# Where the last two residual gates stand, and by how many products the last one is made

## Chip, cores and metric

One NeuronCore of a Trainium2 chip (trn2). The metric is device time in microseconds of one execution of the kernel; lower is better.

## The reference

One encoder layer on 2048 prompt tokens and 64 sample tokens, model width 1024, all in float32. Cut to what matters here:

```python
h = rms_norm(x, g_pre)
vA, bA, cA, zA, q, f, iv, zB, gA, gB = split_cols(h @ w_in)          # ten projections of 1024
yA = (silu(zA) * bA * causal_conv3(cA * vA)) @ w_a_out               # path A
o  = hgrn2_scan(S0, q, k(f), iv, log(fg(f)))                         # path B, chunks of 64
yB = (rms(o) * g_onorm * silu(zB)) @ w_b_out
out = (sigmoid(gA) * yA + sigmoid(gB) * yB) @ w_o
x = x + rms_norm(out, g_post)
gate = sigmoid(rms_norm(x, g_ple) @ w_ple_gate)                      # the residual gate, W_G
x = x + (p @ w_ple_proj) * gate                                      # PLE
```

The results are x, the last two columns of the convolution's input, and the scan's final states, for prompt and sample.

## The kernel before

The 2112 tokens are cut into three blocks of 768, 704 and 640 (`SIZES`), each with two halves (`segs`, 384, 352 and 320 columns). Everything is kept with features on the partitions and tokens in the free dimension, so a tile of a block is 128 x 768, 128 x 704 or 128 x 640, and eight tiles make the width of 1024. Float32 accuracy comes from splitting both operands into a high and a low part (`split`, line 230: a cast on ScalarE, a subtraction on VectorE) and three matmuls, hi·hi, hi·lo, lo·hi. Weights come from HBM as pieces of 256 KB (`load_raw`, on SP's queue). Their low part is either subtracted again or, where it has been stored before (`lows`), loaded with another 256 KB (`split_w`).

Most products of weights and activations are made by seven products instead of eight (Winograd's form of Strassen's method) over 2 x 2 pieces, with the sums S1 to S4 of the weights and T1 to T4 of the activations. There are two forms of this:

- `sgroup` (lines 457 to 459) takes two output blocks at a time, for the ten projections. Sums of the weights are made in the first block, kept in HBM (`sums`) and loaded in the others.
- `in_turn` (lines 608 to 610) makes product after product over four groups g, for W_A, W_B and W_O. The order of the products is `IN_TURN` or `IN_TURN_LATE`; the activations' sums for the next product are made while one runs (`operand_of`); a stage's `sink` takes each quarter of the output. `anew` names the weights whose low part is subtracted and not loaded. The weights' sums for these stages are made ahead by `prepare_sums`, in pieces hung between other work.

The residual gate, W_G, is made by plain products in all three blocks (`gemm`, `gemm_by_k`, lines 646 to 648). PLE is plain too (`ple`, lines 1318 to 1320).

A block runs through path B (eight heads, `path_b`), path A (`path_a`), W_A, W_B, W_O, the norm after W_O (`final_norm`), the gate (`final_gate`). `final_norm` sums squares of W_O's output, makes the first factor (`rms`: transposes on TensorE, a reduction, the power -0.5 on POOL in line 704, transposes back), adds x, makes the second factor likewise and multiplies by `g_ple`, which gives the gate's operand h.

Steps that should run beside matmuls are hung on hooks: `spread_out` gives plans of how many steps run after each group of matmuls. An instruction within `placed()` comes no earlier on its engine than the last matmul written before it. A DMA given to `paced` waits for that matmul. The remaining order on each engine is a planner's, by the order of writing, readiness and estimated costs. Large activation tiles share one ring of 48 (`rt`).

In the first and the middle block the norm is hung between the next block's first seven groups of projections (`LEAD`), and the gate follows right behind them, ahead of the next block's path B. In the last block there is no next block. There the norm is split by halves, each with its own factors; the first half's norm is begun within the last product of W_O and goes on beside PLE, and the second half's is hung between the first half's gate:

```python
norms = [final_norm(bl, [s], xo, acc, h2, None, s is segs[1]) for s in segs]
...
spread_out((norms[0], (2, 2, 1, 0, 1, 1, 4, 4)), (norms[1], (0,) * 6 + (1, 1) + (1, 1, 1, 0, 0, 1, 0, 1, 4, 4)))
run(ple(bl, ph, kept, spare=range(KB)))
run(gate[0], 2)
...
run(gate[1])
```

Of the kernel before, what the change touches and what calls it, by code (L numbers as in the profile page):

```python
# [18 lines left out]
P = 128  # L19
# [75 lines left out]
def hybrid_step(  # L95
# [193 lines left out]
    def load_w(idx, anew=False):  # L289

        parts = []
        for half_ in range(2):
            raw = load_raw(w_blk[idx, half_])
            with tc.high_priority():
                parts.append(split_w(raw, None if anew else (idx, half_)))
        return parts
# [3 lines left out]
    last, hooks, copies, adds, ahead, evicted, freed, powers, means = [None], [], [None], [None], [], [], [], [], []  # L300
# [31 lines left out]
    sums = {}  # L332
# [9 lines left out]
    def kept_w(i1, i2, name, anew=False, spread=False):  # L342
# [7 lines left out]
        return split_w(load_raw(sums[i1][name]), (i1, name))  # L350
# [24 lines left out]
    def prepare_sums(firsts, shared=False, pieces=False):  # L375
# [33 lines left out]
        for n, i1 in enumerate(firsts):  # L409
# [4 lines left out]
            if i1 >= W_O:  # L414
# [17 lines left out]
            if more and W_B <= i1 < W_O:  # L432
                nxt = load(firsts[n + 1])
# [3 lines left out]
            if more:  # L437
                if not W_B <= i1 < W_O:
                    nxt = load(firsts[n + 1])
                yield  # L440
# [132 lines left out]
    def in_turn(stages, operand):  # L573
# [15 lines left out]
        for i, (st, n) in enumerate(todo):  # L589
# [4 lines left out]
            for g in range(KH):  # L594
# [33 lines left out]
                elif what in ("p5", "p7"):  # L628
# [3 lines left out]
                    with behind_all(ahead):  # L632
                        V.tensor_tensor(p57, p57, t, ALU.add)
                        st["sink"](g, 1, 1, u2, p57)
# [18 lines left out]
    def gemm(idx, act, segs, anew=False):  # L653
# [23 lines left out]
    def gemm_by_k(idxs, act, segs, anew=False):  # L677
# [22 lines left out]
    def rstd_of(ms_ap, out_ap, scale):  # L700
        scaled = V.tensor_scalar(out_ap, ms_ap, scale, EPS, ALU.mult, ALU.add).ins
        means[:] = [scaled]
# [26 lines left out]
    def rms(acc, out, segs, hasten=False):  # L729
# [4 lines left out]
        for sg, col in zip(segs, cols):  # L734
            if hasten:
                ahead[:] = [V.tensor_copy(out[:, cols_of(sg)], spread(col, sg["n"])).ins]
            else:
                A.copy(out[:, cols_of(sg)], spread(col, sg["n"]))
# [490 lines left out]
    def path_b(bl, hc, first, kept, fills, hs, lead_sums=None):  # L1229
# [9 lines left out]
        for hd in range(NH):  # L1239
# [7 lines left out]
            piece = lead_sums and partial(next, lead_sums, None)  # L1247
# [162 lines left out]
    def out_in_turn(mg, xo, acc, last):  # L1410


        stage = dict(idx=W_O, order=IN_TURN if last else IN_TURN_LATE, raw=mg, anew=())
        if last:
            xo.extend(rt() for _ in range(KB))
        begun = set()

        def sink(g, c, h, x, y):
            if not last and c == 0 and h == 0:
                xo.append(rt())  # L1420
            v = half((xo if last or c == 0 else stage["mid"])[g + c * KH * last], h)
            into(v, x, y)
            if last:
                sum_squares(int(h in begun), v, half(acc, h), hn())
                begun.add(h)
# [4 lines left out]
    def final_norm(bl, segs, xo, acc, h2, kept, ask_ahead=False):  # L1430
# [3 lines left out]
        c = slice(segs[0]["off"], segs[-1]["off"] + hn())  # L1434
        n = len(segs) * hn()
        acc2, rs, rs2 = rt(), rt(), rt()
        xks = []

        def fetch():
            j = len(xks)  # L1440
            if j < KB:
                xks.append(rt())
                load = G.dma_start(xks[j][:, c], x_fm[j * P : (j + 1) * P, segs[0]["t0"] : segs[0]["t0"] + n])
                if not bl["last"]:
                    paced(load)

        if kept is not None:
            for j in range(KB):
                sum_squares(j, xo[j], acc, width[0])
                if j % 2:  # L1450
                    yield
        for _ in range(2):
            fetch()
            if kept is not None:
                yield
        for _ in rms(acc, rs, segs, bl["last"]):
            if kept is not None:
                fetch()
            yield
        if ask_ahead:  # L1460
            for _ in range(3):
                fetch()
                fetch()
                yield
        for j in range(KB):
            fetch()
            xj = xo[j][:, c]
            V.scalar_tensor_tensor(xj, xj, g_post[:, j : j + 1], rs[:, c], ALU.mult, ALU.mult)
            V.tensor_tensor(xj, xj, xks[j][:, c], ALU.add)

            for i in (j,) if not bl["last"] else (j - 1,) if 0 < j < KB - 1 else (j - 1, j) if j else ():
                sum_squares(i, xo[i][:, c], acc2[:, c], n)
            yield
        stored = iter(range(0 if kept is None else KB))
# [6 lines left out]
        for _ in rms(acc2, rs2, segs, bl["last"]):  # L1481
# [3 lines left out]
        for j in range(KB):  # L1485
            store(1)
            if len(h2) <= j:
                h2.append((rt(dt=F32R), rt(dt=F32R)))

            for i in (j, j + 1) if j == 0 else (j + 1,):  # L1490
                if i < KB:
                    ts.append(rt())
                    V.scalar_tensor_tensor(ts[i][:, c], xo[i][:, c], g_ple[:, i : i + 1], rs2[:, c], ALU.mult, ALU.mult)
            split(ts[j][:, c], h2[j][0][:, c], h2[j][1][:, c])
            yield

    def final_gate(bl, segs, xo, h2, kept, anew=False, held={}):

        late = []

        def merge(j, t, pj, xj):
            V.tensor_tensor(t[:, c], pj[:, c], t[:, c], ALU.mult)
            V.tensor_tensor(t[:, c], t[:, c], xj[:, c], ALU.add)
            (SP if bl["last"] and j >= KB - 2 else G).dma_start(y_fm[j * P : (j + 1) * P, segs[0]["t0"] : segs[0]["t0"] + len(segs) * hn()], t[:, c])

        c = slice(segs[0]["off"], segs[-1]["off"] + hn())
        for j in range(KB):
            if not bl["last"]:
# [313 lines left out]
```

## Time and profile before

| | |
|---|---|
| median of 3 runs | 2519.85 us (2516.96 to 2520.59) |
| profiled execution | 2516.69 us, its span 2515.0 us |
| TensorE (PE) busy | 2500.4 us, 99% |
| VectorE (DVE) busy | 1887.6 us, 75% |
| ScalarE (ACT) busy | 1491.5 us, 59% |
| GpSimd (POOL) busy | 481.0 us, 19% |
| DMA | 736.17 MB, mean 293 GB/s |

PE is matmuls, PEld weight loads, which overlap them. Lines such as L608 are lines of the kernel. A matmul is shown with its whole way through the pipeline, about 0.3 us for 320 columns, though the next one begins about 0.15 us after it; so the pace is read from starts. An arrow `<-` names what ended the wait before an instruction.

### The profile page before, as it was taken

The page shows a single profiled execution, that of the slowest core. Times are in us where ns is not written, and L with a number is a line of the kernel's source. Part 1 is how long each engine was busy: PE and PEld are TensorE (multiplying, and loading weights), DVE is VectorE, ACT ScalarE, POOL GpSimd, SP SyncE. Part 2 cuts the span into 40 slices and gives each one's busy share as a digit, 9 for nine tenths or more (in the row PEclk, how much of TensorE's full clock was granted, in tenths as well). Part 3 has the DMA queues.
Part 4 walks back from the last instruction along what each step waited for, and adds up shares of the span by engine and source line. Part 5 has one row for each costly group of instructions (what it writes and reads, how often), then busy time and mean ns, then how long its engine had stood idle before and what let it go on. Part 6 is the DMA issues. An engine that isn't in the chain of part 4 may idle for free.

```text
span 2515.0 us, 47257 instructions
## 1 busy us (share of the span) xinstructions
PE 2500.4 (99%) x16302; PEld 2481.1 (99%) x16302; DVE 1887.6 (75%) x3639; ACT 1491.5 (59%) x2902; POOL 481.0 (19%) x819
## 2 busy tenths in 40 slices
PE   9999999999999999999999999999999999999999
PEld 9999999999999999999999999999999999999998
DVE  7889999988867775588885657978357776447967
ACT  6676676554554663466655555677366665546675
POOL 2032222320022021122223221102213221001011
PEclk9999999999999999999999999999999999999999
DMA  8789889997687798788889988979988887889986
GB/s 331 241 310 336 313 297 324 325 325 265 233 333 263 255 331 286 260 272 283 284 279 326 340 290 310 330 264 353 311 270 287 287 292 256 267 257 320 333 271 201
DMA packets 344048, 736.17 MB, mean 293 GB/s; under 512 B 42934, under 2 KB 48368, under 8 KB 343808
## 3 DMA queue, kind: packets, MB, share of 16 engines
q1 hardware_dynamic: 292032, 528.68, 62.3%
q0 software_dynamic: 51776, 204.48, 22.9%
q8 instruction: 128, 2.10, 0.3%
q14 instruction: 112, 0.92, 0.1%
HBM read 531.90 MB, written 201.09 MB: 291 GB/s over the span
## 4 chain that ended last, share of the span: by engine, by line
PE 92%; DVE 3%; DMA 2%; ACT 1%; issue 1%; POOL 0%; SPq 0%; ACTq 0%; DVEq 0%; POOLq 0%
PE pg L457 20%; PE pg L458 20%; PE pg L459 20%; PE pg L609 5%; PE pg L608 5%; PE pg L610 5%; PE pg L648 3%; PE pg L647 3%; PE pg L646 3%; PE pa L1147 1%; PE pa L1115 1%; PE pa L1185 1%; PE pa L1187 1%; DMA raw<-w_blk 1%; PE pa L1318 0%
## 5 line engine op out<-in xcount | busy, mean ns | idle before, releaser
L457 PE MATMUL pg<-r,hi 128*128 128x320 f32 (+2 forms) x3304 | 1074.8, 325 | 1.6 <-DVE r L505 1.6
L458 PE MATMUL pg<-r,hi 128*128 128x320 f32 (+2 forms) x3304 | 1066.9, 323 | 0.0
L459 PE MATMUL pg<-r,lo 128*128 128x384 f32 (+2 forms) x2380 | 775.2, 326 | 0.1
L279 ACT CAST hi<-raw 128x512 fp32r<-128x512 f32 x594 | 366.9, 620 | 441.1 <-PE pg L458 188.5
L457 PEld LDWEIGHTS pg<-r,hi 128*128 128x128 f32 x3304 | 621.0, 188 | 4.0 <-DVE r L505 2.2
L458 PEld LDWEIGHTS pg<-r,hi 128*128 128x128 f32 x3304 | 621.6, 188 | 0.0
L459 PEld LDWEIGHTS pg<-r,lo 128*128 128x128 f32 x2380 | 447.0, 188 | 0.6 <-DMA lo<-low 0.4
L230 ACT CAST hi<-raw 128x512 fp32r<-128x512 f32 x380 | 234.3, 621 | 192.3 <-PE pg L458 60.1
L459 PE MATMUL pg<-r,s 128*128 128x352 f32 (+1 forms) x924 | 291.7, 316 | 0.2 <-DMA s<-low 0.2
L609 PE MATMUL pg<-r,hi 128*128 128x320 f32 (+2 forms) x864 | 277.5, 322 | 0.1
L608 PE MATMUL pg<-r,hi 128*128 128x320 f32 (+2 forms) x864 | 274.9, 322 | 0.0
L230 DVE TENSOR_TENSOR lo<-raw,hi 128x512 fp32r<-128x512 f32 x296 | 202.4, 686 | 79.8 <-ACT hi L230 78.0
L230 DVE TENSOR_TENSOR r<-r,r 128x320 fp32r<-128x320 f32 (+7 forms) x350 | 206.1, 607 | 41.5 <-ACT r L230 40.4
L230 ACT CAST r<-r 128x320 fp32r<-128x320 f32 (+7 forms) x350 | 183.8, 556 | 39.5 <-DVE r L1358 9.0
L610 PE MATMUL pg<-r,lo 128*128 128x352 f32 (+2 forms) x564 | 180.7, 321 | 0.3 <-DMA lo<-low 0.3
L230 ACT CAST hi<-s 128x512 fp32r<-128x512 f32 x164 | 101.9, 623 | 126.1 <-PE pg L458 99.8
L459 PEld LDWEIGHTS pg<-r,s 128*128 128x128 f32 x924 | 173.6, 188 | 0.5 <-DMA s<-low 0.5
L647 PE MATMUL pg<-r,hi 128*128 128x384 f32 (+2 forms) x512 | 167.4, 328 | 0.1
L646 PE MATMUL pg<-r,hi 128*128 128x384 f32 (+2 forms) x512 | 165.6, 327 | 0.2 <-ACT hi L279 0.2
L609 PEld LDWEIGHTS pg<-r,hi 128*128 128x128 f32 x864 | 162.2, 188 | 1.7 <-DVE r L230 1.3
L608 PEld LDWEIGHTS pg<-r,hi 128*128 128x128 f32 x864 | 161.2, 188 | 1.3 <-ACT r L230 0.8
L471 ACT COPY hf<-pg 128x352 f32<-128x352 f32 (+2 forms) x354 | 157.1, 447 | 0.8 <-PE pg L459 0.7
(383 smaller groups left out, 4154.8 us busy)
## 6 DMA issues: line engine op xcount, KB each, us to landing
raw<-w_blk SPq DMA_DIRECT2D x579, 256.0 KB, 4.5
raw<-S SPq DMA_DIRECT2D x436, 256.0 KB, 4.1
lo<-low SPq DMA_DIRECT2D x355, 256.0 KB, 4.3
s<-low SPq DMA_DIRECT2D x239, 256.0 KB, 4.6
low<-lo SPq DMA_DIRECT2D x207, 256.0 KB, 3.9
S<-s SPq DMA_DIRECT2D x152, 256.0 KB, 4.2
low<-r POOLq DMA_DIRECT2D x50, 256.0 KB, 4.6
r<-w_blk POOLq DMA_DIRECT2D x48, 256.0 KB, 6.9
```

Source lines behind the costliest of these rows:

```text
L230: return A.copy(hi, src).ins, V.tensor_tensor(lo, src, hi.bitcast(F32), ALU.subtract).ins
L279: A.copy(hi, raw)
L457: add(hi[:, k, :], xhi, start=start and k == 0, stop=False)
L458: add(hi[:, k, :], xlo, start=False, stop=False)
L459: last[0] = add(lo[:, k, :], xhi, start=False, stop=k == KH - 1).ins
L471: copied = A.copy(got[n], ps[bank])
L608: add(hi[:, k, :], xhi, start=start and k == 0, stop=False)
L609: add(hi[:, k, :], xlo, start=False, stop=False)
L610: last[0] = add(lo[:, k, :], xhi, start=False, stop=k == KH - 1).ins
L646: T.matmul(ps, hi[:, k % 4, :], xhi[:, c], start=k == ks[0], stop=False)
L647: T.matmul(ps, hi[:, k % 4, :], xlo[:, c], start=False, stop=False)
L648: last[0] = T.matmul(ps, lo[:, k % 4, :], xhi[:, c], start=False, stop=k == ks[-1]).ins
```

## The change

The last two blocks' gates both stand behind the last W_O.

- The middle block's norm stays where it was, but its h is stored to HBM (`keep_h`) and not split. During W_O of the last block it is loaded again (`ask_h`) and split (`split_held`).
- Behind the last W_O the middle block's gate runs, plain as before (`final_gate(..., by_k=True)`), with the low part of every second half of a weight subtracted anew. The last block's norm, now over whole rows of 640, hangs between its products; then PLE of the last block follows.
- The last block's gate is a stage of `in_turn` with seven products (`gate_in_turn`). Its sink takes the sigmoid, the product with PLE's tile and the sum with x; some of these on POOL. The weights' sums for it are prepared in the last block's path A by `prepare_sums`.
- In the last block's path A the low parts of S1 and S2 are subtracted and not loaded (`fresh`), and so are those of A11 and A12 in its W_O. W_O's sink no longer sums squares.

The core of the diff:

```diff
-        return split_w(load_raw(sums[i1][name]), (i1, name))
+        return split_w(load_raw(sums[i1][name]), None if name in fresh else (i1, name), name in fresh)
...
-            if i1 >= W_O:
+            if W_O <= i1 < W_G:
...
-        stage = dict(idx=W_O, order=IN_TURN if last else IN_TURN_LATE, raw=mg, anew=())
+        stage = dict(idx=W_O, order=IN_TURN if last else IN_TURN_LATE, raw=mg, anew=("A11", "A12") if last else ())
...
-            v = half((xo if last or c == 0 else stage["mid"])[g + c * KH * last], h)
-            into(v, x, y)
-            if last:
-                sum_squares(int(h in begun), v, half(acc, h), hn())
-                begun.add(h)
+            into(half((xo if last or c == 0 else stage["mid"])[g + c * KH * last], h), x, y)
...
+    def final_norm(bl, xo, acc, kept, take, early):
+        segs = bl["segs"]
+        acc2, xks = None, []
+
+        def fetch():
+            j = len(xks)
+            if j < KB:
+                xks.append(rt())
+                paced(G.dma_start(xks[j], x_fm[j * P : (j + 1) * P, bl["t0"] : bl["t0"] + bl["n"]]))
+
+        for j in range(KB):
+            sum_squares(j, xo[j], acc, width[0])
+            if j % 2:
+                yield
+        for _ in range(2):
+            fetch()
+            yield
+        rs = rt()
+        for _ in rms(acc, rs, segs):
+            fetch()
+            yield
+        for j in range(KB):
+            fetch()
+            V.scalar_tensor_tensor(xo[j], xo[j], g_post[:, j : j + 1], rs, ALU.mult, ALU.mult)
+            V.tensor_tensor(xo[j], xo[j], xks[j], ALU.add)
+            if j == 0:
+                acc2 = rt()
+            sum_squares(j, xo[j], acc2, width[0])
+            yield
...
+            while len(ts) < min(j + 1 + early, KB):
+                i = len(ts)
+                ts.append(rt())
+                V.scalar_tensor_tensor(ts[i], xo[i], g_ple[:, i : i + 1], rs2, ALU.mult, ALU.mult)
+            take(j, ts[j])
+            yield
...
+    def keep_h(kept, j, t):
+        kept["h", j] = spill("h", j)
+        paced(G.dma_start(kept["h", j], t))
+
+    def ask_h(kept, held):
+        for j in range(KB):
+            t = rt(dt=F32R)
+            paced(G.dma_start(t.bitcast(F32), kept["h", j]))
+            held.append(t)
+            yield
+
+    def split_held(held):
+        for j in range(KB):
+            hi = rt(dt=F32R)
+            split(held[j].bitcast(F32), hi, held[j])
+            held[j] = hi, held[j]
+            yield
+
+    def final_gate(bl, h2, kept, by_k=False):
+        segs = bl["segs"]
+        for j in range(KB):
+            if by_k and j < 2:
+                both = gemm_by_k([W_G, W_G + 1], h2, segs, (1,)) if j == 0 else both
+                pss = both[j]
             else:
+                pss = gemm(W_G + j, h2, segs, (1,) if by_k else ())
+            xj, pj, t = reload(kept["x", j]), reload(kept["p", j]), rt()
             for s, ps in zip(segs, pss):
+                A.activation(t[:, cols_of(s)], ps, AF.Sigmoid)
+            V.tensor_tensor(t, pj, t, ALU.mult)
+            V.tensor_tensor(t, t, xj, ALU.add)
+            G.dma_start(y_fm[j * P : (j + 1) * P, bl["t0"] : bl["t0"] + bl["n"]], t)
+            yield
+
+    def gate_in_turn(bl, h2, xs, kept):
+        def sink(g, c, h, x, y):
+            j, s = g + c * KH, whole(x, y)
+            t = hf() if y is None else s
+            A.activation(t, s, AF.Sigmoid)
+            v = half(kept["p", j], h)
+            (G if c == h == 0 else V).tensor_tensor(v, v, t, ALU.mult)
+            (V if (c, h) == (0, 1) else G).tensor_tensor(v, v, half(xs[j], h), ALU.add)
+            t0 = bl["segs"][h]["t0"]
+            (SP if (c, h) == (0, 1) and g >= 2 else G).dma_start(y_fm[j * P : (j + 1) * P, t0 : t0 + hn()], v)
+
+        return dict(idx=W_G, order=IN_TURN, raw=h2, anew=("A11", "A12"), sink=sink)
...
-        ahead_of = (*range(W_A, W_A + KH), W_O, W_O + 1) if first else None if bl["last"] else range(W_B, W_B + KH)
+        ahead_of = (*range(W_A, W_A + KH), W_O, W_O + 1) if first else range(W_G, W_G + KH) if bl["last"] else range(W_B, W_B + KH)
...
+        fresh[:] = ("S1", "S2") if bl["last"] else ()
         path_a(bl, hc, a, first, side(rows), ready)
+        fresh.clear()
...
+            elif bl["last"] and idx == W_O and 1 <= n <= 4:
+                run(asked, 2)
+            elif bl["last"] and (idx, n) == (W_O, 5):
+                a_first.clear()
+                norm = sized(bl, final_norm(bl, xo, rt(), kept, lambda j, t: h2.append(t), 0))
+                spread_out(
+                    (held_parts, (1,) * 4 + (2, 2)),
+                    (norm, (0,) * 4 + (1,) * 4 + (2, 1, 0, 1, 1, 1, 2, 1, 2, 1, 1, 0) + (1, 1, 2, 1, 2, 1, 1)),
+                    (sized(bl, ask_p()), (0,) * 16 + (1, 0, 0, 1)),
+                    (sized(bl, first_halves()), (0,) * 24 + (1,) * 4),
+                )
...
-            run(final_gate(bl, segs, xo, h2, kept))
+            if first:
+                run(final_gate(bl, h2, kept))
+            else:
+                held = []
+                asked, held_parts = (sized(bl, gen) for gen in (ask_h(kept, held), split_held(held)))
         else:
-            gate = [final_gate(bl, [s], xo, h2, kept, anew=s is segs[1], held={} if s is segs[1] else {0: 0, 1: 0, 2: 0, 3: 2, 4: 0, 5: 4}) for s in segs]
-            spread_out((norms[0], (2, 2, 1, 0, 1, 1, 4, 4)), (norms[1], (0,) * 6 + (1, 1) + (1, 1, 1, 0, 0, 1, 0, 1, 4, 4)))
+            run(sized(blocks[bi - 1], final_gate(blocks[bi - 1], held, kepts[bi - 1], True)))
             run(ple(bl, ph, kept, spare=range(KB)))
-            run(gate[0], 2)
-            with behind_all(copies[:1]):
-                run(norms[1], KB)
-            run(gate[0])
             assert not hooks
-            run(gate[1])
+            for idx, n in in_turn([gate_in_turn(bl, h2, xo, kept)], a_first):
+                assert not hooks
```

129 lines of the change are left out of this document (31 added, 98 removed).

## Prediction

> **What bounds the kernel now.** I read the page first, then the busy times by stage, TensorE's waits over the last 300 us, the chain there, and single rows of the end. The page:
>
> ```profile
> span 2515.0 us, 47257 instructions
> PE 2500.4 (99%) x16302; PEld 2481.1 (99%) x16302; DVE 1887.6 (75%) x3639; ACT 1491.5 (59%) x2902; POOL 481.0 (19%) x819
> PEclk9999999999999999999999999999999999999999
> ```
>
> TensorE is never idle for long and its clock is granted in full throughout. So there are two ways to be faster: fewer matmuls, or closing the 14.6 us in which PE is idle. Busy times by stage (us of the stretch, then each engine's busy time with its instruction count, clock, DMA share, GB/s):
>
> ```profile
> core 0: us, PE busy (x) PEld busy (x) DVE busy (x) ACT busy (x) POOL busy (x), PEclk, DMA share, GB/s
> 1771.00:1833.40 62.40, 62.40 (x388) 62.16 (x388) 15.46 (x19) 17.65 (x35) 13.57 (x25) 1.00 0.87 287
> 2086.00:2283.00 197.00, 197.00 (x1351) 197.00 (x1350) 104.91 (x187) 101.62 (x191) 12.41 (x30) 1.00 0.82 259
> 1325.00:1517.00 192.00, 191.78 (x1192) 191.18 (x1191) 115.36 (x220) 104.37 (x212) 47.14 (x99) 1.00 0.93 321
> 2333.00:2383.00 50.00, 49.72 (x338) 49.14 (x337) 45.20 (x107) 32.06 (x70) 3.97 (x8) 1.00 0.95 333
> 2433.50:2449.80 16.30, 15.51 (x107) 14.76 (x105) 12.96 (x32) 13.00 (x36) 0.88 (x1) 1.00 0.82 267
> 2449.80:2510.50 60.70, 59.32 (x393) 57.42 (x393) 47.84 (x103) 33.57 (x70) 12.95 (x22) 1.00 0.65 217
> 2510.50:2515.00 4.50, 0.00 (x1) 0.00 (x0) 0.98 (x2) 0.44 (x1) 0.00 (x0) 1.00 0.10 36
> ```
>
> In order: the middle block's gate, path A of the last block and of the middle one, W_B of the last block, then what follows the last W_O: PLE, gate, end. The end of the kernel is 16.3 + 60.7 + 4.5 = 81.5 us. It should be nearer its arithmetic than it is, because the norm that feeds the gate has little beside it. TensorE's waits after 2200 us (total, times, longest), and two pieces of the chain (start, us):
>
> ```profile
> PE pa L712 <- POOL cols L704: 1.5, 2, 0.8
> PE pg L610 <- DMA lo<-low: 0.3, 1, 0.3
> PE pa L724 <- DVE r L747: 0.2, 1, 0.2
> PE pg L646 <- ACT hi L279: 0.2, 1, 0.2
> PE pg L648 <- DVE lo L230: 0.2, 1, 0.2
> ```
>
> ```profile
> 2449.85 1.12 POOL cols L704
> 2466.41 1.56 ACT r L746 x4
> ```
>
> The norms' powers on POOL, their squares and sums come last there. The pace of matmuls of 320 columns, and the end:
>
> ```profile
> 2505.03 0.31 PE L646 MATMUL pg<-r,hi 128*128 128x320 f32 x1
> 2509.01 0.31 PE L646 MATMUL pg<-r,hi 128*128 128x320 f32 x1
> 2510.20 0.31 PE L648 MATMUL pg<-r,lo 128*128 128x320 f32 x1
> 2510.54 0.44 ACT L1519 ACTIVATE r<-pg 128x320 f32<-128x320 f32 x1 [3.10 <-PE pg L648]
> 2511.01 0.49 DVE L1502 TENSOR_TENSOR r<-r,r 128x320 f32<-128x320 f32 x1 [2.52 <-ACT r L1519]
> 2511.54 0.49 DVE L1503 TENSOR_TENSOR r<-r,r 128x320 f32<-128x320 f32 x1
> 2512.06 0.34 SPq L1504 DMA_DIRECT2D y_fm<-r  x1
> ```
>
> Nine triples (hi·hi, hi·lo, lo·hi) lie between the first two rows: 3.98 us / 27 = 0.1474 us a matmul. A row's 0.31 us is its time in the pipeline, not its price.
>
> **Matmuls removed.** The last gate has 8 output blocks x 2 halves x 8 k x 3 = 384 matmuls; by seven products it has 7 x 4 x 4 x 3 = 336. Removed: 48 x 0.1474 = 7.1 us. PLE keeps 96, the middle gate its 384 of 352 columns (62.4 us, moved, with no idle PE in it), and the norms their 24 transposes (three to a half, there and back, two factors). One of those, of 128 columns, costs between 128/320 of 0.1474 and the whole of it, 1.4 to 3.5 us for all; I take 2.7. They stand in the old end and in the new one, so the choice only shifts what is called a wait.
>
> **Waits removed.** The old end should take 480 x 0.1474 + 2.7 = 73.4 us of PE against 77.0 measured, so 3.6 us are waits and restarts. With 62 us of another block's matmuls in hand while the last norm runs, these go. What is late next is below.
>
> **End.** The last sink gains one VectorE addition ahead of the sigmoid (u2 and the bank, of 320 columns like the two 0.49 above): +0.5 us.
>
> So the end becomes 96 x 0.1474 + 336 x 0.1474 + 2.7 + 5.0 = 71.4 us against 81.5: **-10.1 us** before new waits.
>
> **New waits: VectorE behind the middle gate.** Prices:
>
> ```profile
> L1502 DVE TENSOR_TENSOR r<-r,r 128x704 f32<-128x704 f32 x7 | 6.3, 893 | 40.9 <-DMA r<-p 24.3 <-ACT r L1519 16.6
> L230 DVE TENSOR_TENSOR lo<-raw,hi 128x512 fp32r<-128x512 f32 x7 | 4.8, 690 | 10.7 <-ACT hi L230 10.7
> L230 DVE TENSOR_TENSOR r<-r,r 128x640 fp32r<-128x640 f32 x1 | 0.8, 825 | 0.0
> L810 DVE SCALAR_TENSOR_TENSOR r<-r,vec,r 128x640 f32<-128x640 f32 x2 | 1.8, 879 | 0.0
> L498 DVE TENSOR_TENSOR hf<-r,pg 128x320 f32<-128x320 f32 x16 | 7.7, 481 | 8.4 <-PE pg L610 8.2
> L725 DVE TENSOR_REDUCE cols<-pa 128x3 f32<-128x384 f32 x4 | 2.0, 550 | 0.4 <-PE pa L724 0.4
> ```
>
> Steps are hung on hooks, one per 24 matmuls of the middle gate (3.9 us). The first factor is asked for at the eighth and tenth of them (31 us in) and is there at about 32.5. TensorE reaches the third of the seven products, whose operand T2 takes most subtractions, at 62.4 + 14.2 (PLE) + 1.4 (half the transposes) + 14.2 (two products) = 92. In those 59.5 us VectorE must do: eight norm steps of 0.88 + 2 x 0.83, less one addition, 19.4; five of the gate's merges, 2 x 0.89 each, 8.9; four splits of its weights 2.8; p 1.7; reductions 1.5; eight products with g_ple 7.0; the four halves of B11 1.9; A11 and A12 split, 5.5; B21 1.9 and T2 9.6 (five operations of 0.48 on each of four tiles). That is 60.2 us: booked full. In W_B of the last block VectorE was busy 45.2 of 50 us and PE lost 0.3 us, so 90% is carried. At 90% the list takes 66.9 us and TensorE waits 7.4 us; at 100% it waits 0.7. I take 3.0, nearer to the full share, since most of the list is ready early and only the order is in question, and keep 0.5 to 7.5.
>
> **New waits elsewhere.** In path A of the last block VectorE gets 16 sums and 16 splits (preparation) and 32 splits (S1, S2 anew): 64 x 0.69 = 44 us on 104.9 of 197. It has room. DMA gains 48 pieces of 256 KB and loses 32, about 4.2 MB in 197 us or 21 GB/s on 259. Path A of the middle block already carries the like preparation (115.4 of 192 us, 321 GB/s) and PE lost 0.2 us. The POOL queue, which issues those pieces, was busy 12.4 us there and would stay under the middle block's 47.1. In the seven products of W_G, five read 2 x 4 x 256 KB in 12 x 4 x 0.1474 = 7.1 us, 296 GB/s, where 333 were carried.
>
> The tighter place is where the middle gate is taken from. The norm ahead of it now stores h, 8 pieces of 352 KB, beside the x it stored already, and where it does so the DMA engines are full:
>
> ```profile
> 1751.00:1761.00 10.00, 10.00 (x71) 10.00 (x70) 8.69 (x14) 6.84 (x13) 1.62 (x3) 1.00 1.03 379
> ```
>
> Eight pieces are 2.9 MB, 7.6 us of that rate. They take the place of the middle gate's first weights, x and p, which were fetched there ahead; behind them comes path B's weights instead of a gate with 62 us of slack. VectorE is relieved at that place by h's eight splits, which is no gain on PE. If the weights of one group are late by what the stores take beyond what they replace, TensorE waits up to half of the 7.6 us, 4; if the stores only drag on behind, nothing. For all of this paragraph and the one before 1.0 us, from 0 to 5, nearer to nothing since PE was full in this row at the full DMA.
>
> **Sum.** -10.1 + 3.0 + 1.0 = -6.1 us. The profiled execution took 2516.69 us (1.69 around its span) and would take 2510.6; the median of the three runs shown is 3.2 above it, and on that base it is 2519.85 - 6.1 = 2513.7.
>
> **Rivals.**
>
> *The gain is spent at the hand-over.* VectorE takes the 90% pace or worse and TensorE waits 5 to 10 us before PLE, B11 or T2. For it: the list is as long as its time, and PLE's operands are queued with it; the stores of h can add their 4. Against it: W_B. Net 0 to -5: 2515 to 2520.
>
> *The last norm's x waits in the POOL queue, and the change is slower.* In the middle gate now:
>
> ```profile
> L1344 POOL DMA_DIRECT2D r<-x x8 | 4.4, 548 | 34.0 <-DMA y_fm<-r 31.7 <-DMA g__5193_22423<-r 2.3
> ```
>
> POOL stood 31.7 us there until a stored y gave its buffer back. With the last norm's x asked for on the same queue, its steps would come at the pace of the gate's outputs, one per 62.4 / 8 = 7.8 us instead of one per 3.4. Each step so held is 4.4 us; three of them (13 us) outweigh the gain of 10.1, four give 17.6 - 6.1 = +11.5, 2531. Against it: that stage held the next block's 28 operand tiles of the 48 in the ring, which the end of the kernel doesn't.
>
> *POOL's share of the sinks holds VectorE up.* The new sinks put 16 operations of 320 columns on POOL, eight of them while T2 is made. What the trace has of the two engines side by side:
>
> ```profile
> 1894.01 1.86 POOL L1083 COPY r<-r 128x640 f32<-128x640 f32 x1 [2.51 <-DMA r<-tk]
> L1083 POOL COPY r<-r 128x640 f32<-128x640 f32 x8 | 7.3, 912 | 18.1 <-DMA r<-tk 18.1
> 151.45 0.93 DVE L230 TENSOR_TENSOR lo<-s,hi 128x512 fp32r<-128x512 f32 x1 [1.42 <-ACT hi L230]
> L704 POOL TENSOR_TENSOR ms<-ms,mhalf 128x4 f32<-128x4 f32 x24 | 29.4, 1225 | 28.0 <-DVE ms L701 19.7 <-PE pg L459 8.2
> ```
>
> The copy took twice its mean in the first row, and a split 0.93 us against 0.69 in the third. One POOL operation of 320 columns lies between half the copy, 0.46, and the dearest power, 1.23. If VectorE stands still for all eight, T2 is 3.7 to 9.8 us later: net -2.4 to +3.7, 2517 to 2524. Against it: in the busy first row POOL was the one that lost. [...]
>
> That seven products are not made is no rival: the loops are written out.
>
> **How the numbers follow.** Forecast 0.60; spent at the hand-over 0.19; x in POOL's queue 0.11; POOL against VectorE 0.10. About 0.2% (5 us) is what a measurement of this kernel can tell from no change. The forecast passes it where all new waits together stay under 5.1 us. Faster: 0.60. Same: 0.19 and half of the last rival, 0.24. Slower: 0.11 and the other half, 0.16. The range: all gain and no wait from the lower runs (2516.96 - 10.1 = 2507) to the first rival's end and into the third's (2521). It leaves out the POOL queue's case and some of the third, under 0.2.
>
> **What would show it.** Right: 48 matmuls fewer; the middle gate's lines between the last W_O and the last PLE with PE full in it; no wait on POOL's powers; from the end of W_O to the end of the span 62.4 us of the middle gate and 71 to 77 more. Wrong: a TensorE wait over 5 us on VectorE at PLE or at the first three products; POOL waiting on y_fm for most of the middle gate, with the norm's steps 7.8 us apart; a VectorE over 95% in the seven products of W_G; a loss in the last block's path A or B of over 2 us.

## The result, and the profile after

The kernel after takes 2521.65 us (median of 22 runs, 2518.07 to 2526.21) against 2516.71 of the kernel before on the same chips (22 runs). The ratio is 1.0017, with a 95% interval of 1.001 to 1.0023: slower by 0.17%, 4.3 us, where 6.1 us less were forecast. That is just under the 0.2% which the prediction named as the bound of what can be told from no change, with the whole interval on the slow side. The page of the profiled execution (2522.08 us):

```profile
span 2520.4 us, 47301 instructions
PE 2495.2 (99%) x16254; PEld 2476.1 (98%) x16254; DVE 1943.3 (77%) x3699; ACT 1504.2 (60%) x2926; POOL 530.9 (21%) x891
```

The 48 matmuls are gone (16302 to 16254) and TensorE is busy 5.2 us less, yet the span is 5.4 us longer. So TensorE idles some 10 us more. Busy times by stage, first two stretches of the kernel before, then the kernel after: from the last block's first projections to the end of W_O, middle gate, PLE, last gate, end.

```profile
core 0: us, PE busy (x) PEld busy (x) DVE busy (x) ACT busy (x) POOL busy (x), PEclk, DMA share, GB/s
1681.20:1771.10 89.90, 89.25 (x614) 88.96 (x613) 67.31 (x106) 63.27 (x117) 18.00 (x30) 1.00 0.92 332
1833.40:2433.50 600.10, 597.72 (x4267) 591.34 (x4267) 409.99 (x874) 363.14 (x696) 86.23 (x143) 1.00 0.86 285
...
1680.30:2374.30 694.00, 687.07 (x4875) 679.85 (x4874) 507.60 (x1030) 427.24 (x814) 138.70 (x231) 1.00 0.86 302
2374.30:2444.20 69.90, 65.84 (x405) 65.23 (x404) 46.61 (x65) 29.88 (x56) 17.08 (x31) 0.98 0.67 230
2444.20:2458.80 14.60, 14.60 (x103) 14.59 (x103) 11.14 (x16) 11.19 (x29) 1.94 (x2) 1.00 0.75 234
2458.80:2513.80 55.00, 52.26 (x338) 50.64 (x336) 41.60 (x79) 34.49 (x79) 22.77 (x30) 0.97 0.68 224
2513.80:2520.40 6.60, 0.03 (x1) 0.00 (x0) 2.37 (x5) 0.73 (x2) 0.16 (x1) 0.70 0.28 101
```

Against the prediction's terms: the stretch to the end of W_O, without the gate that stood in it, went from 89.9 + 600.1 = 690.0 to 694.0 us (+4.0 where 1.0 was allowed). The middle gate went from 62.4 to 69.9 (+7.5). PLE and the seven products take 14.6 + 55.0 = 69.6, where the forecast had 66.4 with all the transposes in it (+3.2), the end 6.6 instead of 5.0 (+1.6). That is 16.3 us of losses against a gain of 10.1; what stands ahead of the last block is 0.9 us shorter, and 16.3 - 10.1 - 0.9 = 5.3 is the longer span but for rounding. TensorE's waits after 1600 us of the kernel after (total, times, longest):

```profile
PE pa L722 <- DVE r L742: 3.6, 1, 3.6
PE pg L459 <- DMA s<-low: 2.1, 1, 2.1
PE pg L609 <- DVE r L230: 1.5, 3, 0.9
PE pg L608 <- ACT r L230: 1.4, 2, 0.9
```

The first is the transposes of the last norm's second factor, within the middle gate; the second a weight piece of path B in the last block, where h is being stored; the third and fourth are nearly all T2, the operand of the third of the seven products (0.53, 0.89, 0.87 and 0.46 us, one behind the other). They are fewer than the losses. The rest is the clock, in stretches of 5 us of the kernel after:

```profile
2435.00:2440.00 5.00, 2.12 (x9) 2.15 (x10) 3.67 (x6) 3.04 (x6) 2.00 (x4) 0.79 0.98 314
2440.00:2445.00 5.00, 5.00 (x29) 5.00 (x29) 2.60 (x6) 1.18 (x3) 1.36 (x2) 0.86 0.46 165
...
2475.00:2480.00 5.00, 2.79 (x12) 2.07 (x12) 4.96 (x6) 2.46 (x7) 4.23 (x6) 0.89 0.53 200
2480.00:2485.00 5.00, 5.00 (x29) 5.00 (x29) 4.28 (x11) 3.84 (x10) 0.52 (x1) 0.77 0.77 245
2485.00:2490.00 5.00, 5.00 (x36) 5.00 (x36) 3.75 (x9) 4.65 (x12) 0.00 (x0) 1.00 0.80 260
```

PEclk, the granted clock, falls behind the 3.6 us wait and behind T2's four short ones. The first pair lacks 0.21 x 5 + 0.14 x 5 = 1.75 us of full-speed time, the second 1.7 as well; at half speed that is some 3.5 us each. The starts of the matmuls agree: in the second place 12 of 320 columns begin in the 3.36 us from 2478.97 to 2482.33, 0.28 us apart, where the full pace is 0.147. So each of the two places costs its waits and some 1.7 us of clock.

### The profile page after: what moved, and what is told of

It is laid out like the page before. It is cut to its first block, busy times and chain, and to the rows that moved or that the text cites. A ratio compares the mean times of both kernels' runs of the same rounds, so it can differ in the third digit from the quotient of the medians.

```text
span 2520.4 us, 47301 instructions
## 1 busy us (share of the span) xinstructions
PE 2495.2 (99%) x16254; PEld 2476.1 (98%) x16254; DVE 1943.3 (77%) x3699; ACT 1504.2 (60%) x2926; POOL 530.9 (21%) x891
## 5 line engine op out<-in xcount | busy, mean ns | idle before, releaser
L457 PE MATMUL pg<-r,hi 128*128 128x320 f32 (+2 forms) x3304 | 1074.7, 325 | 1.7 <-DVE r L505 1.7
L458 PE MATMUL pg<-r,hi 128*128 128x320 f32 (+2 forms) x3304 | 1066.8, 323 | 0.0
L457 PEld LDWEIGHTS pg<-r,hi 128*128 128x128 f32 x3304 | 621.0, 188 | 4.0 <-DVE r L505 2.2
L458 PEld LDWEIGHTS pg<-r,hi 128*128 128x128 f32 x3304 | 621.6, 188 | 0.0
L609 PE MATMUL pg<-r,hi 128*128 128x320 f32 (+2 forms) x976 | 313.3, 322 | 1.6 <-DVE r L230 1.5
L608 PE MATMUL pg<-r,hi 128*128 128x320 f32 (+2 forms) x976 | 310.4, 321 | 1.4 <-ACT r L230 1.4
L230 DVE TENSOR_TENSOR lo<-raw,hi 128x512 fp32r<-128x512 f32 x320 | 219.4, 687 | 93.5 <-ACT hi L230 88.6
L230 DVE TENSOR_TENSOR r<-r,r 128x320 fp32r<-128x320 f32 (+7 forms) x374 | 221.0, 611 | 44.1 <-ACT r L230 43.3
L230 ACT CAST r<-r 128x320 fp32r<-128x320 f32 (+7 forms) x374 | 195.9, 557 | 34.1 <-DVE r L1353 8.8
L610 PE MATMUL pg<-r,lo 128*128 128x320 f32 (+2 forms) x656 | 209.2, 319 | 0.0
L609 PEld LDWEIGHTS pg<-r,hi 128*128 128x128 f32 x976 | 183.9, 189 | 4.1 <-DVE r L230 3.8
L608 PEld LDWEIGHTS pg<-r,hi 128*128 128x128 f32 x976 | 182.9, 188 | 3.3 <-ACT r L230 2.9
L230 DVE TENSOR_TENSOR lo<-s,hi 128x512 fp32r<-128x512 f32 x164 | 114.1, 696 | 45.0 <-ACT hi L230 40.6
L505 DVE TENSOR_TENSOR r<-hf,pg 128x128 f32<-128x128 f32 (+5 forms) x164 | 64.3, 411 | 95.7 <-PE pg L459 95.4
```

The lines of the kernel that those rows point to most:

```text
L230: return A.copy(hi, src).ins, V.tensor_tensor(lo, src, hi.bitcast(F32), ALU.subtract).ins
L457: add(hi[:, k, :], xhi, start=start and k == 0, stop=False)
L458: add(hi[:, k, :], xlo, start=False, stop=False)
L505: V.tensor_tensor(dst, x, y, ALU.add)
L608: add(hi[:, k, :], xhi, start=start and k == 0, stop=False)
L609: add(hi[:, k, :], xlo, start=False, stop=False)
```

## The experiments

Ratios are to the kernel before, run beside each. A thousandth is 2.5 us, about as much as an interval reaches to either side, so small effects are read from the stages too.

**Loads asked ahead (e1).** Why does the second factor come late? POOL's queue and VectorE in the middle gate of the kernel after (start, duration, operation, idle time before it and what ended it):

```profile
2394.67 0.54 POOL L1431 DMA_DIRECT2D r<-x_fm  x1 [28.26 <-PE pg L647]
...
2409.31 0.55 POOL L1509 DMA_DIRECT2D y_fm<-r  x1 [6.87 <-ACT r L1506]
2409.84 0.55 POOL L1431 DMA_DIRECT2D r<-x_fm  x1
...
2410.92 0.55 POOL L1339 DMA_DIRECT2D r<-p  x1
...
2406.92 0.89 DVE L1507 TENSOR_TENSOR r<-r,r 128x704 f32<-128x704 f32 x1 [6.49 <-DMA r<-p]
2416.71 0.89 DVE L1507 TENSOR_TENSOR r<-r,r 128x704 f32<-128x704 f32 x1 [2.71 <-DMA r<-p]
```

POOL stood 28.3 us at the first of the last norm's loads of x (x_fm), which is paced, that is, waits for a matmul. The gate's own p and x of its third output stand behind it. Later the next p, and the norm's x too, stand behind the store of the output before (y_fm), which waits for that output. So the gate's merges lag, VectorE waits for p (6.5 and 2.7 us) and is then full when the norm's sums and the factor are due.

```diff
+            while len(asked) < min(j + 1 + 2 * by_k, KB):
+                asked.append((reload(kept["x", len(asked)]), reload(kept["p", len(asked)])))
...
-            xj, pj, t = reload(kept["x", j]), reload(kept["p", j]), rt()
+            (xj, pj), t = asked[j], rt()
```

> The loads of x and p for the middle gate are asked for two outputs ahead, so they stand in POOL's queue in front of the last norm's paced loads of x and not behind them. Theory (POOL's queue): the merges, and with them the norm, were late because p came late; the middle gate's 69.8 us become 62.5 to 64.5, the 3.6 us wait before the second factor's transposes goes, the clock stays full there, and the kernel is 5 to 7 us faster than the changed one, 2515 to 2517 where the kernel before is 2516.7. Rival (VectorE is simply booked full from the first factor on): the wait stays within 1 us of what it was and the time within 1.5 us.

1.0021 (1.0012 to 1.0029): no gain, where 5 to 7 us were expected. The wait for the factor is gone and the middle gate takes 66.9 us, but there is a wait in its place, again in TensorE's waits:

```profile
PE pg L647 <- DMA lo<-low: 2.0, 1, 2.0
```

Five pairs of p and x are now asked without pacing from 2362.5 on, and the low part of a weight at the gate's start comes late. So the order of POOL's queue is the cause of the late factor, but loads that are not paced move the loss.

**POOL's share later (e2).** The first four sinks' products and sums on POOL are put behind the third product:

```diff
+            if c == h == 0:
+                def rest(v=v, t=t, j=j):
+                    paced(G.tensor_tensor(v, v, t, ALU.mult))
+                    G.tensor_tensor(v, v, half(xs[j], 0), ALU.add)
...
+                rests.append(rest)
+                return
```

> The eight POOL operations of the first sink of the seven-product gate run one product later, beside a stage in which VectorE has little to do. Theory (POOL and VectorE shut each other out): the subtractions for T2 take 0.48 us again and not 0.9 to 1.3, TensorE's four waits there (2.7 us) go and the clock with them: 4 us less than the changed kernel. Rival (T2 is late because VectorE is booked): the durations fall but T2 still waits, under 1.5 us gained. Second rival: the waits move to the stage where POOL now works.

1.0004 (0.9995 to 1.0013), 0.13% or 3.3 us less than the kernel after, 4 expected. The two intervals still touch, so the stage is the better witness. T2's waits are gone and the seven products take 49.9 us instead of 55.0. First the rows of both engines in the kernel after while T2 is made, then T2's operations grouped, of after (one row) and of e2:

```profile
2469.06 0.87 POOL L1520 TENSOR_TENSOR r<-r,hf 128x320 f32<-128x320 f32 x1 [21.17 <-ACT hf L1518]
2470.01 1.02 POOL L1521 TENSOR_TENSOR r<-r,r 128x320 f32<-128x320 f32 x1
...
2467.70 0.48 DVE L562 TENSOR_TENSOR hf<-r,r 128x320 f32<-128x320 f32 x1
2469.35 0.93 DVE L230 TENSOR_TENSOR r<-hf,r 128x320 fp32r<-128x320 f32 x1 [0.64 <-ACT r L230]
2470.20 1.17 DVE L562 TENSOR_TENSOR hf<-r,r 128x320 f32<-128x320 f32 x1
```

```profile
L562 DVE TENSOR_TENSOR hf<-r,r 128x320 f32<-128x320 f32 x4 | 4.0, 993 | 0.0
...
L562 DVE TENSOR_TENSOR hf<-r,r 128x320 f32<-128x320 f32 x4 | 1.9, 485 | 0.0
```

VectorE's 0.48 us become 0.93 to 1.17 in these rows while a POOL operation runs, 0.99 in the mean of T2's first sum, and 0.485 again without POOL. POOL's take 0.87 to 1.02 us here and 0.87 to 1.05 in the later products, so VectorE is the one that loses time. That the two shut each other out, as the expectation's theory has it, is shown here for VectorE alone.

**One h stored (e3).** Only the first of the eight tiles of the middle block's h is stored and then read eight times, which leaves out the true h in the other seven.

```diff
-        paced(G.dma_start(kept["h", j], t))
+        if j == 0:
...
+            paced(G.dma_start(kept["h", 0], t))
...
-            paced(G.dma_start(t.bitcast(F32), kept["h", j]))
+            paced(G.dma_start(t.bitcast(F32), kept["h", 0]))
```

> Only the first of the eight h tiles of the middle block is stored, and is read eight times, so the middle gate computes with a wrong operand; seven stores of 352 KB are left out. Theory (the stores fall where DMA is full): the 2.1 us wait on a weight's low part just behind the middle norm goes, 2 to 3 us less than the changed kernel. Rival (that wait is path B's first group without stored low parts made anew, whatever the stores): it stays, and the time is the same within 1 us.

1.0006 (0.9997 to 1.0015), 0.11% or 2.8 us less than after. By the starts of its matmuls (1679.05 to 2368.86) the stretch to the end of W_O is 689.8 us, as the 690.0 of the kernel before; some of that is lost again in the middle gate, where the wait for the second factor is 4.4 us in this execution. Where h was stored, ten us by stage, first in after, then in e3:

```profile
1770.00:1780.00 10.00, 7.86 (x53) 7.60 (x53) 2.62 (x4) 3.08 (x6) 2.15 (x4) 1.00 1.03 401
...
1770.00:1780.00 10.00, 10.00 (x70) 10.00 (x69) 3.14 (x7) 5.39 (x12) 0.54 (x1) 1.00 1.02 362
```

The 2.1 us wait for a low part of a weights' sum comes from the stores. A full share alone does not make it: it is 1.03 with the wait and 1.02 without.

**e1 and e2 together (e4).** The edit is the sum of both.

> Loads two outputs ahead and POOL's operations one product later, together. If the two waits are separate, the gains add up: 8.5 to 11 us less than the changed kernel, 2511 to 2513 where the kernel before is 2516.7. If the one wait only hides the other (TensorE stands earlier or later for the same VectorE work), the sum is nearer to the larger of the two, 5 to 7 us, and the kernel is level with the one before.

1.0002 (0.9993 to 1.001), 2516.6 us where 2511 to 2513 were expected: 3.8 us less than after, little more than e2 alone. The first weights of the gate are waited for again (1.8 us), as in e1, which is why e5 paces the loads.

**Loads one output ahead, paced (e5).**

```diff
+            while len(asked) < min(j + 1 + by_k, KB):
+                i, late = len(asked), by_k and len(asked) > 1
+                asked.append((reload(kept["x", i], late), reload(kept["p", i], late)))
```

> As the first experiment, but only one output ahead, and from the third output on each pair of loads waits for the matmuls of the output before the one ahead of it, so the five pairs no longer come at once while W_O's last weights are loaded. Theory (POOL's queue, and the first experiment only moved the wait to the weights' low parts): the 3.6 us wait before the transposes stays away and the 2.0 us wait for a low part at the gate's begin goes too; the middle gate takes 62.5 to 65 us and the kernel is 4 to 7 us faster than the changed one. Rival (VectorE's list is too long in any order of loads): the wait before the transposes comes back, 1 us or less gained.

0.9998 (0.9989 to 1.0008), 0.19% or 4.8 us less than after. Middle gate and last gate of e5, by stage:

```profile
2375.00:2439.00 64.00, 64.00 (x403) 63.64 (x403) 47.31 (x66) 30.99 (x57) 18.35 (x31) 1.00 0.75 257
...
2453.90:2508.40 54.50, 52.08 (x337) 50.42 (x335) 41.39 (x78) 34.56 (x78) 22.89 (x30) 0.97 0.68 226
```

TensorE is full throughout the middle gate, with the same work on VectorE (47.3 against 46.6 us busy). So VectorE had the room; the work came to it too late. The seven products still lose their time (54.5 us), as e5 leaves POOL's operations where they were.

**The first group's low parts anew (e6).**

```diff
-            sgroup(FF * 8 + hd, IV * 8 + hd, hc, sink_f, first, anew=hd == 0 and not bl["last"])
+            sgroup(FF * 8 + hd, IV * 8 + hd, hc, sink_f, first, anew=hd == 0)
```

> The last block's first group of projections behind the middle norm subtracts its weights' low parts anew, as the middle block's does; five loads of 256 KB less where h is stored. All h stores stay. Theory (there DMA is short of room): the 2.1 us wait for a low part behind the norm goes, 2 to 3 us less than the changed kernel, as with one h store. Rival (the stores delay every load, the raw weights too): a wait for raw weights takes its place, within 1 us of the changed kernel.

1.0021 (1.0012 to 1.0029): no gain by itself, where 2 to 3 us were expected. The one 2.1 us wait became three for another low part, 1.6 in all.

**Three of them (e7: e2, e5 and e6).**

> Three changes together: paced loads one output ahead, POOL's operations one product later, the first group's low parts anew. If the three waits are separate and are the cause of the missed forecast, the matmuls saved come through: 2508 to 2512 where the kernel before is 2517, ratio 0.9965 to 0.998. If a fourth cause carries the loss, the ratio stays at 0.999 or above.

0.9971 (0.9961 to 0.9981), 2510.3 us, as expected: faster than the kernel before. By stage as above:

```profile
1680.50:2374.00 693.50, 686.82 (x4875) 679.79 (x4874) 508.07 (x1030) 425.92 (x812) 137.52 (x231) 1.00 0.87 302
2374.00:2438.00 64.00, 64.00 (x404) 63.68 (x403) 47.11 (x66) 30.88 (x58) 18.53 (x31) 1.00 0.74 257
2438.00:2452.60 14.60, 14.60 (x102) 14.59 (x102) 11.20 (x16) 11.30 (x29) 1.13 (x2) 1.00 0.69 219
2452.60:2502.40 49.80, 49.77 (x338) 49.18 (x336) 41.89 (x78) 34.31 (x78) 22.58 (x30) 1.00 0.73 247
```

The two places give 5.9 and 5.2 us against after, the first stretch 0.5; less 0.3 elsewhere that is the 11.3 us between the spans (2520.4 and 2509.1). What the third edit adds to the other two was not measured alone.

**All sinks on VectorE (e8).** The same question as e2 by another way: the work stays at its place, and VectorE does POOL's part as well.

```diff
-            (G if c == h == 0 else V).tensor_tensor(v, v, t, ALU.mult)
-            (V if (c, h) == (0, 1) else G).tensor_tensor(v, v, half(xs[j], h), ALU.add)
+            V.tensor_tensor(v, v, t, ALU.mult)
+            V.tensor_tensor(v, v, half(xs[j], h), ALU.add)
```

> All products and sums of the last gate's sinks on VectorE, none on POOL: 16 operations more on VectorE, eight of them while T2 is made. Theory (POOL and VectorE shut each other out, so an operation on POOL costs VectorE as much as its own): T2's subtractions take 0.48 us each, but eight operations of 0.48 stand among them, 3.9 us against the about 5 us that POOL's eight cost; the waits before T2 shrink from 2.7 us to 1 to 2.5, and the kernel is within 2 us of the changed one. Rival (VectorE is what counts and POOL relieves it): the waits grow by 3 us or more and the kernel is 4 us slower than the changed one.

1.001 (1.0001 to 1.0019), about 1.8 us less than after, which the intervals do not separate. But no TensorE wait is left in the seven products (50.1 us), as with e2; the wait for the second factor stayed, at 4.7 us in this execution. T2's sum in e8:

```profile
L562 DVE TENSOR_TENSOR hf<-r,r 128x320 f32<-128x320 f32 x4 | 1.9, 483 | 0.0
```

I had expected 1 to 2.5 us of waits to stay. Eight more operations of 0.48 us on VectorE while T2 is made cost less than the same eight on POOL. So the cause is not VectorE's load but POOL beside it.

**h stored later (e9: e7, and the eight stores of h go one to a group into the first head of the last block's path B).**

```diff
-        paced(G.dma_start(kept["h", j], t))
+        late_h.append((kept["h", j], t))
...
+                if late and hd == 0:
+                    for slot in range(8):
+                        at(slot, store_h)
```

> The three changes together, and the eight stores of h moved from the end of the middle norm to the first head of the last block's path B, one per group of matmuls. Theory (what is left of the loss ahead of path A is the stores of h, as the run with one store showed): the waits for low parts around the block's first group, 1.7 us and up to 0.8 later, go; 1.5 to 3 us less than the three changes together, 2507.5 to 2509 where the kernel before is 2517. Rival (the eight tiles of h are missed in the ring while they wait): path B's first heads wait for buffers and the kernel is 1 us slower or more than the three together.

2507.8 us, ratio 0.9966 (0.9953 to 0.9978): the fastest version, 0.34% under the kernel before. Against e7's 0.9971 the intervals overlap, so the step itself is not shown by the time. By stage, from the last block's first projections to the end of W_O, and the middle gate:

```profile
1684.90:2376.30 691.40, 686.37 (x4874) 679.64 (x4873) 507.68 (x1030) 426.86 (x812) 137.24 (x231) 1.00 0.88 303
2376.30:2440.20 63.90, 63.90 (x405) 63.65 (x404) 46.90 (x65) 30.89 (x58) 17.67 (x30) 1.00 0.74 254
```

The first stretch is 2.1 us shorter than in e7, and the waits for low parts, 2.4 us there, are gone from it; the last gate takes 49.7 us as in e7. (This execution took 2512.92 us, above its median: at the end of the middle block TensorE waited 1.7 us, and PEclk was 0.66 from 1638 to 1643 us.)

**The last gate plain (e10: e7 with the last gate by plain products and h split by halves; the sums for seven products are still prepared, and left unused).**

```diff
-            for idx, n in in_turn([gate_in_turn(bl, h2, xo, kept)], a_first):
+            for j in range(KB):
+                pss, t = gemm(W_G + j, h2, segs, (1,)), rt()
...
```

> The three changes together, but the last gate by plain products, with h split behind the norm; the weights' sums for it are still prepared and not used. This is the move without the seven products. Theory (48 matmuls at 0.147 us are worth 7.1 us and nothing else hangs on the form): 7 us more than the three together, 2517 to 2518, level with the kernel before. If the seven products cost something of their own that the plain ones don't (the longer sink at the end, VectorE's operands), the difference is 4 to 6 us; if the plain ones wait for h's split, it is 8 or more.

0.9992 (0.9983 to 1.0001). Last gate of e10, whose end takes 5.0 us:

```profile
2454.20:2510.70 56.50, 56.49 (x384) 55.98 (x383) 24.30 (x44) 18.32 (x38) 6.46 (x12) 1.00 0.36 110
```

Against e7 the gate is 56.5 - 49.8 = 6.7 us longer and the end 1.7 shorter; by the ratios e7 is 0.21%, 5.3 us, faster. That is the net worth of the seven products, in the expected 4 to 6 us for a form with a cost of its own (the longer end). The move of the middle gate alone leaves 0.0008, 2 us, with an interval that includes no change; e10 still prepares the sums that it does not use, and a plain version without them was not measured.

**The end of the last product first (e11: e7 with a higher priority for the last quarter's sum and sigmoid).** The end of the kernel after on VectorE, the last matmul ending at 2513.8:

```profile
2514.09 0.49 DVE L1520 TENSOR_TENSOR r<-r,hf 128x320 f32<-128x320 f32 x1 [0.60 <-ACT hf L1518]
2514.62 0.49 DVE L1521 TENSOR_TENSOR r<-r,r 128x320 f32<-128x320 f32 x1
2515.03 0.48 DVE L498 TENSOR_TENSOR hf<-r,pg 128x320 f32<-128x320 f32 x1
```

The last sum (line 498) waits behind the group before, whose product waits for its sigmoid.

```diff
+            with tc.high_priority() if (c, h) == (0, 1) else nullcontext():
+                s = whole(x, y)
+                t = hf() if y is None else s
+                A.activation(t, s, AF.Sigmoid)
```

> The three changes together, with the sum and the sigmoid of the last product's sinks given precedence on their engines over the earlier group's product and sum. From the last matmul to the end of the span the three together take 6.7 us, where the kernel before took 4.5 and 5.0 was forecast. Theory (the last sum waits behind the earlier group's sink on VectorE): 0.5 to 1.2 us less, 5.5 to 6.2 us for the end. Rival (the end is the store's landing): no change in the end, time the same within 0.5 us.

0.9971 (0.996 to 0.9983), end 6.6 us: nothing changed, since the order on VectorE stayed the same. The experiment says nothing of what the end could be; that stays open.

**Low parts loaded again (e12: e9 with the low parts of S1, S2, A11 and A12 loaded and not subtracted anew).**

```diff
-        fresh[:] = ("S1", "S2") if bl["last"] else ()
+        fresh[:] = ()
...
-        stage = dict(idx=W_O, order=IN_TURN if last else IN_TURN_LATE, raw=mg, anew=("A11", "A12") if last else ())
+        stage = dict(idx=W_O, order=IN_TURN if last else IN_TURN_LATE, raw=mg, anew=())
```

> The version with the stores of h moved, with one part of the change undone: in the last block's path A the low parts of S1 and S2, and in its W_O those of A11 and A12, are loaded again and not subtracted; 40 loads of 256 KB more (10.5 MB), 40 subtractions of 0.69 us less on VectorE. Theory (path A has room on both sides, and W_O ran at the same loads in the kernel before): the same within 1.5 us as the version with the stores moved, 2507 to 2510. Rival (the loads collide with the sums' preparation and with h's loads during W_O): waits for low parts of 2 us or more in all, 2 us slower or more.

0.9996 (0.9987 to 1.0005), 2516.46 us: 0.30%, 7.5 us, slower than e9, where I had expected nothing. TensorE's waits:

```profile
PE pg L459 <- DMA lo<-low: 2.9, 1, 2.9
PE pg L610 <- DMA s<-low: 1.9, 1, 1.9
```

Such waits are not in e9. The 5.5 us of these and two smaller ones (0.4 and 0.3), and the clock behind the second (PEclk 0.66 over 5 us, 1.7 us), make most of it. The two halves of the edit were not undone one by one. So this part, which looks like a trifle beside the rest, is needed: without it the weights come late. Which transfers delay them was not tested.

## Why the prediction was wrong, point by point

**Right: what is removed.** 48 matmuls went, and in e10 against e7 they are worth 6.7 us where 7.1 were worked out. The powers on POOL are no longer waited for. Given its operands, the middle gate takes 64 us (e5, e7, e9), its old 62.4 and the transposes of the norm beside it; and PLE and the seven products take 14.6 + 49.8 = 64.4, where 66.4 was forecast with all transposes in it. Middle gate and end of the kernel together took 62.4 + 81.5 = 143.9 us before and take 64.0 + 64.4 + 6.7 = 135.1 in e7: 8.8 of the 10.1 us, and the longer end is the rest.

**The step that failed: "VectorE behind the middle gate", +3.0 us (0.5 to 7.5).** The two waits are 3.6 and 2.7 us. The stretches they lie in grew by 7.5 and 3.2 us, 10.7 in all, over the upper end; beside the waits that is 1.7 us of clock in each, and some 1.6 us of transposes that were forecast in the second stretch and stand in the first. The reason given was wrong as well. The list "booked full" could be carried: e5 did it with no wait in the gate, and e8 made T2 without a wait with eight operations more on VectorE. The waits for T2 came from POOL, the next point. What I did not see is the first part of the path: my list began at the eighth hook as if VectorE could do its share from then on, but the loads it needed stood in POOL's queue behind a load that waits for a matmul, and then behind the stores. The list also had one deadline, T2 at 92 us, while the transposes of the second factor stand within the gate: TensorE waited for them at 2434.3, 60 us in. VectorE was idle when it should have worked ahead. Here are stretches of the middle gate, first three of after, then two of e5, whose gate begins 0.8 us later:

```profile
2410.00:2420.00 10.00, 10.00 (x65) 10.00 (x64) 7.29 (x11) 4.16 (x8) 2.31 (x5) 1.00 0.67 228
2420.00:2430.00 10.00, 10.00 (x64) 10.00 (x63) 8.93 (x13) 3.97 (x7) 4.15 (x9) 1.00 0.89 312
2430.00:2435.00 5.00, 4.29 (x27) 4.00 (x25) 5.00 (x7) 1.34 (x3) 2.21 (x5) 1.00 0.81 270
...
2410.00:2420.00 10.00, 10.00 (x64) 10.00 (x63) 10.00 (x15) 3.96 (x7) 3.20 (x6) 1.00 0.82 269
2420.00:2430.00 10.00, 10.00 (x64) 10.00 (x63) 9.97 (x15) 4.90 (x9) 3.40 (x8) 1.00 0.74 252
```

VectorE is busy 16.2 of the first 20 us in after and 20.0 in e5, and after then needs all of the last 5 us, in which TensorE begins to wait. The rival "x waits in the POOL queue" had the right place and half of the mechanism: the norm's x did stand behind a store of the gate's output (the row at 2409.84, behind 6.9 us), but the gate's p stood there too, and behind the norm's x, and it was p that VectorE waited for. Its price, 11.5 us on the slow side, was too high.

**"POOL's share of the sinks holds VectorE up"** was a rival at 0.10, and it came true with 2.7 us of waits and 1.7 of clock, within its 3.7 to 9.8. I had given it little weight since a copy on POOL was what lost in the row shown. In the sinks VectorE lost (T2's first sum took 0.99 us beside POOL's operations, 0.485 in e2 and 0.483 in e8), with T2's queue behind it.

**"New waits elsewhere", +1.0 us (0 to 5),** was 4.0, within its range: "nearer to nothing" was the wrong end. The row that made me choose it, PE full at a DMA share of 1.03, lay ahead of a gate of 62 us of plain products; path B's weights are due there now. e3 shows the stores of h as the cause: 2.8 us by the ratio, the whole 4.0 in the stretch itself. The term also rested on the low parts made anew, which the prediction counted as work for VectorE with room to spare and as bytes; e12 shows that without them e9 is 7.5 us slower, waiting for weights, so they were a condition of that term, which the prediction does not say.

**"End", +0.5 us,** was 2.1 (4.5 to 6.6): the addition of 0.48 us was costed alone, and the last sum waits 1.2 us for the group before. No experiment reached it.

**Not in the sum at all: the clock.** The page of before shows it in full throughout, so I priced waits by their length. Each of the two places cost some 1.7 us more, 3.4 us in all.

So three terms make up the difference from -6.1 to +5.4 but for rounding: the hand-over 7.7 more than forecast (the clock, which had no term, included), elsewhere 3.0, the end 1.6, less 0.9 ahead of the last block. With the first of these undone and the second partly (e9, whose stretch to the end of W_O is 1.4 us over the kernel before), the change is worth 0.34%, 8.6 us, 2.5 more than the forecast.

## What to carry to other kernels

Before a stage is given new work, write down its queues in order of issue, not only its busy times: one paced load, which waited 28.3 us for its matmul, held every later load on POOL's queue here, and the engine that seemed to have time ahead had no operands to use it on. An elementwise operation moved from a busy VectorE to POOL was no relief here: VectorE's own sums beside it took 0.99 us and not 0.485 (after against e2), so compare with leaving it there. Behind waits of TensorE like those here allow for a half-clock stretch, of 1.7 us: it followed one wait of 3.6 us, one of 1.9 us and four of 0.5 to 0.9 us within 4.7 us, and not one of 2.1 us and one of 2.9 us.

## What the runs showed of the hardware that I had not expected

The length of a wait alone did not tell here whether TensorE's clock drops. It halved for about 3.5 us behind one wait of 3.6 us (PEclk 0.79 and 0.86 in two stretches of 5 us) and behind four of 0.5 to 0.9 us (2.7 us within 4.7; PEclk 0.89 and 0.77). The 2.1 us wait of the kernel after left it at full speed (PEclk 1.00 from 1770 to 1780). And in one execution, e12's, a 2.9 us wait left it at full speed (the first pair of stretches) and a shorter one, of 1.9 us, did not (the second pair):

```profile
2067.00:2072.00 5.00, 2.07 (x15) 1.80 (x14) 1.87 (x4) 0.85 (x2) 0.76 (x2) 1.00 0.96 307
2072.00:2077.00 5.00, 5.00 (x36) 5.00 (x36) 1.81 (x4) 4.33 (x8) 0.00 (x0) 1.00 0.71 221
...
2368.00:2373.00 5.00, 3.14 (x22) 2.88 (x21) 3.58 (x7) 2.18 (x4) 0.00 (x0) 1.00 1.03 386
2373.00:2378.00 5.00, 5.00 (x24) 5.00 (x25) 3.02 (x6) 3.66 (x6) 0.00 (x0) 0.66 0.88 280
```

What else decides it, no run here shows: none moved a wait by itself.

An operation of 320 columns on POOL took 0.87 to 1.05 us in the kernel after, near the upper end of the 0.46 to 1.23 that the prediction set.
